# Moving weight sums, plane stores and a Silu, and a last norm by columns, in a hybrid decoder layer

## The chip, the core and the metric

The kernel runs on one core of one Trainium2 chip. The metric is the device time of one execution in microseconds (us). Engines are named as in the profile: PE is TensorE's matmul and PEld its weight load, DVE is VectorE, ACT is ScalarE, POOL is GpSimd, SP is SyncE, which issues most DMAs. A small q behind a name (ACTq, SPq) is that engine's issuing of DMAs.

## The reference

One decoder layer over 1024 tokens with 1024 features, all in float32: a half-step SwiGLU (FFN1), a mixer of three gated branches, and a second half-step SwiGLU (FFN2), each between two RMS norms.

```python
def swiglu(u, w_in, w_out):
    gate, up = jnp.split(u @ w_in, 2, axis=-1)      # w_in 1024 x 5632
    return (jax.nn.silu(gate) * up) @ w_out         # w_out 2816 x 1024
...
h = x
f1 = swiglu(rms_norm(h, ffn1_pre_g), ffn1_w_in, ffn1_w_out)
h = h + 0.5 * rms_norm(f1, ffn1_post_g)
u = rms_norm(h, mix_pre_g)
p_rwkv, p_swa, q_mem, gate_logits = _split(u @ w_in, IN_SIZES)
y_a = rwkv7_mix(p_rwkv, ...)                  # recurrence over tokens, 8 heads of 64
y_b = sliding_window_gqa_sinks(...)           # window of 128, 8 query and 2 key heads
y_c = memory_cross_attention(...)             # 256 memory tokens, 4 heads of 128
g_a, g_b, g_c = _split(sigmoid(gate_logits + gate_b), (D, D, D))
merged = g_a * (y_a @ w_branch[0]) + g_b * (y_b @ w_branch[1]) + g_c * (y_c @ w_branch[2])
h = h + rms_norm(merged @ w_out, mix_post_g)
f2 = swiglu(rms_norm(h, ffn2_pre_g), ffn2_w_in, ffn2_w_out)
h = h + 0.5 * rms_norm(f2, ffn2_post_g)
```

## The kernel before

Activations lie with features on the 128 partitions and tokens along the free dimension, in two halves of 512 tokens. Every product is made of three matmuls (`mm3`, L330 to L332): each factor is split into a high part (`w_hi`, a cast on ACT, L264) and a low part (`w_lo`, a subtraction on DVE, L266), and high x high, high x low and low x high are added in PSUM. Weights come as 128x512 tiles `w_raw` of 256 KB, loaded on SP in the order in which they are used (`raw`, L255); five such tiles exist, and eight operands (pairs of `w_hi` and `w_lo`) are made ahead (`prefetch`).

Both feed-forward products use a Strassen-like scheme with seven products of half-size blocks instead of eight. For the first product (`ffn_in`) the factors of the activations are sums of quarters (`factors_*`), and the sums of the input weights are made on DVE in place (`operands`, L285 to L291). Each of the 22 pairs j, a strip of the gate and one of the up half, takes seven block products, b11, b21, t2, t1, t3, b22 and t4 in the code. For the first 9 pairs of FFN1 and the first 13 of FFN2 (`FIRST`) the first two of the seven, which need only half of the tokens, are made early (`ffn_in_gate`) while the rest of the norm is still being made; their results `m1` and `g` go to DRAM (`first_d`) and are loaded again in the pair itself (L599, L600). These are called ahead pairs (`ahead`): they have five products left, 60 matmuls, where a later pair has 84. In a pair, `u1` and `m5` (L608) read PSUM on DVE in an ahead pair and on ACT in a later one; `up` (L621) reads it on DVE; then come the Silu of the second half `g1` (L625), for an ahead pair also the Silu of the reloaded `g0` (L629), and the products with `up` and `m1`. TensorE cannot add the next product to a bank before `u1`, `m5` or `up` has read it.

For the second product (`ffn_outs`) the seven forms of the hidden activations are made from every two pairs (`out_forms`, L567 to L570) and go to DRAM (`form_d`). Its weights need sums of blocks as well. There are 11 sets (`KP`), each of four DVE instructions on four 256 KB tiles `ws` (L555 to L558); a set is loaded on SP from the output weights (L553) and stored to `sum_d` (L560), from where `ffn_outs` later loads it like other weights. One set is made in every even pair.

In the RWKV stage (`rwkv_prep`) DVE and ACT prepare six planes for each of four head pairs while TensorE projects; `raw` copies (L825) on ACT bring a projection from PSUM. Four PSUM banks hold two projections, so TensorE starts the next but one only when the copy of the older one has been made. The planes and `bonus` go to DRAM from ACT's queue (L978, L979), as 64-element pieces.

Attention runs block by block (`attention`); in between, a generator (`filling`) supplies projections of the gates and the first two branches, so that TensorE has matmuls while ACT and DVE do the softmax. Within the tile framework a scheduler orders the instructions of each engine; `high_priority`, `issue_after` and `keep_in_program_order` bind it.

The end of the kernel is the last norm of FFN2 on the last 256 tokens (`post_norm`, `inverse_root`): squares are summed on ACT and DVE, the mean over features is made by two matmuls with a 1/D matrix on 256 columns, ACT and DVE form the inverse root on 128x256 elements, and eight feature tiles are scaled (L752), added to the residual (L755, three of them on POOL) and stored.

Of the kernel before, what the change touches and what calls it, by code (L numbers as in the profile page):

```python
# [17 lines left out]
P = 128  # L18
# [189 lines left out]
class Builder:  # L208
# [41 lines left out]
    def raw(self, ahead):  # L250

        used = self.raw_pos - len(self.raw_ready)
        while self.raw_pos < min(used + 1 + ahead, len(self.raws)):
            t = self.wpool.tile([P, KH, P], F32, tag="w_raw", name="w_raw", bufs=RAWS)
            self.send(t, self.raws[self.raw_pos])  # L255
            self.raw_ready.append(t)
            self.raw_pos += 1
        return self.raw_ready.pop(0)
# [99 lines left out]
    def rstd(self, sqs, width, pool, n, between):  # L358
        nc = self.nc
        V = nc.vector  # L360
        keep = self.tc.keep_in_program_order
        nb = n // P
        ps = self.psum("ps_ms")
        for j in range(nb):
            for i, sq in enumerate(sqs):
                keep(nc.tensor.matmul(ps[:, j : j + 1], sq[:, j * P : (j + 1) * P], self.ones, start=i == 0, stop=i == len(sqs) - 1))
        m, y, hm, q = (pool.tile([P, 4], F32, tag="rs" + t, name="rs" + t, bufs=2)[:, :nb] for t in "myhq")
        with self.tc.high_priority(offset=self.lead):
            V.tensor_scalar(m, ps[:, :nb], 1.0 / width, EPS, ALU.mult, ALU.add)
            V.tensor_scalar(y.bitcast(I32), m.bitcast(I32), 1, None, ALU.logical_shift_right)  # L370
            V.tensor_scalar(y.bitcast(I32), y.bitcast(I32), -1, 0x5F3759DF, ALU.mult, ALU.add)
            V.tensor_scalar(hm, m, -0.5, None, ALU.mult)
            for _ in range(3):
                V.tensor_tensor(q, y, y, ALU.mult)
                V.tensor_tensor(q, q, hm, ALU.mult)
                V.scalar_tensor_tensor(y, q, 1.5, y, ALU.add, ALU.mult)
        between()
        out = self.psum("ps_rs")
        with self.tc.high_priority(offset=self.lead):
            for j in range(nb):  # L380
                keep(nc.tensor.matmul(out[:, j * P : (j + 1) * P], y[:, j : j + 1].broadcast_to([P, P]), self.ident, start=True, stop=True))
        return out, y

# [140 lines left out]
    def ffn_in(self, f, x, form_d, first_d, parts, norm):  # L524

        nc, V = self.nc, self.nc.vector
        with self.tc.tile_pool(reuse_waits="tile", name="ffn_in", bufs=2) as pool:
# [11 lines left out]
            stored = None  # L539
# [7 lines left out]
    def out_sums(self, f, q, pool, loads_behind, sums_behind):  # L547

        nc, V = self.nc, self.nc.vector
        a11, a12, a21, a22 = a = [pool.tile([P, KH, P], F32, tag="ws", name="ws", bufs=4) for _ in range(4)]  # L550
        with self.tc.issue_after(loads_behind.ins):
            for n, t in enumerate(a):
                nc.sync.dma_start(t, self.io[f + "_out"][n, q])  # L553
        with self.tc.issue_after(sums_behind.ins):
# [4 lines left out]
        for n, t in zip(SUMS, (a22, a11, a21, a12)):  # L559
            nc.sync.dma_start(self.sum_d[f][SUMS.index(n), q], t)  # L560

    def out_forms(self, i, first, second, pool, form_d):
# [8 lines left out]
        for n, t in (("b11", b11), ("b21", b21), ("t2", t2), ("t3", t3), ("t4", t4), ("t1", b12), ("b22", b22)):  # L571
            stored = nc.sync.dma_start(form_d[B_FORM[n], i], t)
        return stored
# [16 lines left out]
    def ffn_in_pair(self, f, j, pool, first_d):  # L590
# [4 lines left out]
        if ahead:  # L595
# [3 lines left out]
            self.reload = nc.sync.dma_start(m1, first_d[j, 0])  # L599
# [25 lines left out]
        nc.scalar.activation(g1, g1, ACT.Silu)  # L625
        V.tensor_tensor(g1, g1, up, ALU.mult)
        self.product(px, self.take(name, j), fs["t4"], last=True)
        if ahead:
            nc.scalar.activation(g0, g0, ACT.Silu)  # L629
# [111 lines left out]
    def post_norm(self, acc, part, gcol, xr, pool, save=None):  # L741
# [5 lines left out]
        end = save is self.io["out"]  # L747
        with self.tc.high_priority(offset=self.urgent if end else 0):
            sq = self.sum_squares(xs[KH:] + xs[:KH] if h else xs, pool)
        rs = self.inverse_root(sq, pool, self.between if end else None)  # L750
        for k in range(KD):
            nc.vector.scalar_tensor_tensor(xs[k], xs[k], gcol(k), rs, ALU.mult, ALU.mult)  # L752

            e = nc.gpsimd if end and cols.stop == T and k in (0, 2, 4) else nc.vector
# [109 lines left out]
    def rwkv_prep(self, u, pool, pk_d, ab_d, bonus_d, att_d):  # L864
# [47 lines left out]
        for p in range(NPAIR):  # L912
# [61 lines left out]
            def bonus(p=p, parts=m_parts, m=m, planes=(*bk, at, r, v)):  # L974
                for h, cols, ps in self.head_sums(*parts):
                    V.tensor_tensor(ch(m[:, cols]), ch(ps), planes[4][:, h * 8 : (h + 1) * 8, :], ALU.mult)
                for i, x in enumerate(planes):
                    nc.scalar.dma_start(pk_d[:, :, p, i * C : (i + 1) * C].rearrange("c p t -> p c t"), x)  # L978
                nc.scalar.dma_start(bonus_d[p], m)  # L979
# [198 lines left out]
    def filling(self, u, pool, gate_d, y_d):  # L1178

        for g in range(GATES_EARLY, 22):  # L1180
            ps = {h: self.psum("pgate") for h in (0, 1)}
            yield from self.project_steps(self.strip("win", 24 + g), u, ps)
            self.gate_out(g, ps, pool, gate_d)

# [10 lines left out]
        for g, p in zip(gs, ps):  # L1195
            self.gate_out(g, p, pool, gate_d)
        self.mg = self.u_by_half(F32)
# [188 lines left out]
    def branch(self, i, y, pool, gate_d, mg, halves=(0, 1), between=None):  # L1386

        for q in range(4):
            w = self.strip("wb", 4 * i + q)
            parts = [(h,) for h in halves] if q == 0 or q == 3 and between else [halves]  # L1390
            for n, part in enumerate(parts):
# [3 lines left out]
                yield from self.branch_strip(i, q, w, y, pool, gate_d, mg, part)  # L1395
        return out if between else None
# [31 lines left out]
    def mixer(self, u, cp, close_raws, att_d, gate_d, km_d, vm_d):  # L1428
# [11 lines left out]
        with tc.tile_pool(reuse_waits="tile", name="gates", bufs=2) as gp:  # L1440
# [15 lines left out]
            with tc.tile_pool(reuse_waits="tile", name="att", bufs=1) as ap, tc.tile_pool(name="attw", bufs=2) as pool:  # L1456
# [36 lines left out]
                def turn_values():  # L1493
# [7 lines left out]
                    self.yin = opened.enter_context(tc.tile_pool(reuse_waits="tile", name="yin", bufs=4))  # L1501

# [4 lines left out]
                for _ in self.fills:  # L1507
                    pass
                opened.close()
# [40 lines left out]
    def build(self):  # L1550
        nc, tc, io = self.nc, self.tc, self.io
        with contextlib.ExitStack() as outer, tc.tile_pool(reuse_waits="tile", name="consts", bufs=1) as cp, \
# [4 lines left out]
            self.log_table = False  # L1557
# [10 lines left out]
            self.eps = cp.tile([P, 64], F32, name="eps")[:, :1]  # L1568
            nc.vector.memset(self.eps, EPS * D / P)
            self.ident = cp.tile([P, P], F32, name="ident")  # L1570
# [127 lines left out]
```

## Time and profile before

| what | value |
|---|---|
| median of 3 runs | 2316.37 us (2315.68 to 2319.36) |
| the profiled execution | 2317.92 us, span 2316.2 us |
| mean granted clock of TensorE | 0.994 |
| instructions | 33482 |
| DMA | 417.68 MB, mean 180 GB/s |

FFN1's gates and ahead pairs lie between about 40 and 232 us, its later pairs up to about 470, the RWKV stage between about 760 and 930, attention with the fills between about 1200 and 1510, FFN2's gates and ahead pairs between about 1640 and 1914, and the last norm in the final 15 us.

In the lines of the profile, a group shows the line, engine, operation and tiles (out<-in), the count, the busy time and the mean length of one in ns, and the idle time before it with what ended it. A row of a timeline begins with the start and the length in us, and ends with the idle time before it in brackets. Consecutive instructions of one engine overlap at their ends, so the distance between two starts is less than the length of one.

### The profile page before, as it was taken

To read this page: it belongs to the slowest core of one execution; us is meant where nothing else is said; L and a number is where in the kernel's file an instruction comes from. 1 tells how busy PE (TensorE), PEld (TensorE's weight loads), DVE (VectorE), ACT (ScalarE), POOL (GpSimd) and SP (SyncE) were. 2 spreads that over 40 slices of the span, in tenths; PEclk is the share of its full clock that TensorE was granted. 3 is DMA by queue.
4 is the path that set the end of the run, shared out by engine and by line. 5 is a ranking of instruction groups with operands and counts; after the bars stand their busy time and mean duration, and the time that the engine had idled before them with its cause. 6 is when DMAs were issued, how large, how long until landed. Compare 5 with 4: busy or idle time off the path is not lost. (4 is left out here: it accounts for less than half of the span.)

```text
span 2316.2 us, 33482 instructions
## 1 busy us (share of the span) xinstructions
PE 2263.1 (98%) x11914; PEld 1848.4 (80%) x11914; DVE 1657.5 (72%) x2683; ACT 995.3 (43%) x1844; POOL 94.5 (4%) x134
## 2 busy tenths in 40 slices
PE   8999999999999999999999999999999999999997
PEld 6778888888888777888878887778878778888887
DVE  6988666665688776895645466575999886666576
ACT  5523333454555553223444454335653223345452
POOL 0000000000000000001300000240000000000000
PEclk9999999999999999999999999999999999999998
DMA  7477545586654447325435434554557774558663
GB/s 281 164 258 246 178 151 167 172 294 200 191 164 156 108 119 185 120 100 178 148 128 175 133 97 162 178 186 162 179 191 243 248 243 165 168 193 264 211 194 111
DMA packets 280777, 417.68 MB, mean 180 GB/s; under 512 B 82305, under 2 KB 104321, under 8 KB 280353
## 3 DMA queue, kind: packets, MB, share of 16 engines
q1 hardware_dynamic: 231552, 388.20, 50.9%
q10 hardware_dynamic: 49056, 27.34, 4.3%
q8 instruction: 94, 1.54, 0.3%
q14 instruction: 75, 0.61, 0.1%
HBM read 284.89 MB, written 129.50 MB: 179 GB/s over the span
## 5 line engine op out<-in xcount | busy, mean ns | idle before, releaser
L264 ACT CAST w_hi<-w_raw 128x512 fp32r<-128x512 f32 x594 | 366.7, 619 | 718.8 <-PE px L331 140.4
L266 DVE TENSOR_TENSOR w_lo<-w_raw,w_hi 128x512 fp32r<-128x512 f32 x594 | 414.8, 700 | 214.2 <-ACT w_hi L264 190.4
L331 PE MATMUL po<-u,w_hi 128*128 128x512 f32 (+1 forms) x476 | 181.0, 380 | 0.0
L330 PE MATMUL po<-u,w_hi 128*128 128x512 f32 (+1 forms) x476 | 181.0, 380 | 0.0
L332 PE MATMUL po<-u,w_lo 128*128 128x512 f32 (+1 forms) x476 | 181.0, 380 | 0.0
L330 PE MATMUL pgate<-u,w_hi 128*128 128x512 f32 x384 | 155.5, 405 | 0.0
L332 PE MATMUL pgate<-u,w_lo 128*128 128x512 f32 x384 | 151.3, 394 | 0.0
L331 PE MATMUL pgate<-u,w_hi 128*128 128x512 f32 x384 | 149.8, 390 | 0.0
L330 PE MATMUL px<-f,w_hi 128*128 128x512 f32 x352 | 138.8, 394 | 8.1 <-DVE up L621 4.8
L330 PE MATMUL pz<-u,w_hi 128*128 128x512 f32 x352 | 138.2, 393 | 6.1 <-DVE m L608 5.2
L330 PE MATMUL px<-u,w_hi 128*128 128x512 f32 x352 | 137.2, 390 | 2.9 <-ACT w_hi L264 1.5
L331 PE MATMUL pz<-u,w_hi 128*128 128x512 f32 x352 | 137.9, 392 | 0.0
L332 PE MATMUL pz<-u,w_lo 128*128 128x512 f32 x352 | 137.9, 392 | 0.0
L331 PE MATMUL px<-f,w_hi 128*128 128x512 f32 x352 | 137.2, 390 | 0.0
L332 PE MATMUL px<-f,w_lo 128*128 128x512 f32 x352 | 137.1, 389 | 0.0
L332 PE MATMUL px<-u,w_lo 128*128 128x512 f32 x352 | 137.0, 389 | 0.0
L331 PE MATMUL px<-u,w_hi 128*128 128x512 f32 x352 | 137.0, 389 | 0.0
L413 DVE TENSOR_TENSOR u<-hid,u 128x512 fp32r<-128x512 f32 x114 | 78.4, 690 | 47.1 <-ACT u L412 46.1
L332 PEld LDWEIGHTS po<-u,w_lo 128*128 128x128 f32 x476 | 89.5, 188 | 17.1
L331 PEld LDWEIGHTS po<-u,w_hi 128*128 128x128 f32 x476 | 89.5, 188 | 17.0
L330 PEld LDWEIGHTS po<-u,w_hi 128*128 128x128 f32 x476 | 89.5, 188 | 16.9
L412 ACT CAST u<-hid 128x512 fp32r<-128x512 f32 x114 | 70.7, 620 | 65.3 <-DMA hid<-form_d 57.2
(358 smaller groups left out, 5139.3 us busy)
## 6 DMA issues: line engine op xcount, KB each, us to landing
w_raw<-in_ffn_in SPq DMA_DIRECT2D x220, 256.0 KB
hid<-form_d SPq DMA_DIRECT2D x154, 256.0 KB
w_raw<-in_win SPq DMA_DIRECT2D x112, 256.0 KB
ws<-in_ffn_out SPq DMA_DIRECT2D x88, 256.0 KB
form_d<-g SPq DMA_DIRECT2D x88, 256.0 KB
ffn_sum_d<-ws SPq DMA_DIRECT2D x88, 256.0 KB
w_raw<-ffn_sum_d SPq DMA_DIRECT2D x88, 256.0 KB
form_d<-h SPq DMA_DIRECT2D x66, 256.0 KB
```

Source lines behind the costliest of these rows:

```text
L264: self.nc.scalar.copy(hi, x)
L266: self.nc.vector.tensor_tensor(lo, x, hi.bitcast(F32), ALU.subtract)
L330: mm(out, wh, xh, start=first, stop=False, **kw)
L331: mm(out, wh, xl, start=False, stop=False, **kw)
L332: mm(out, wl, xh, start=False, stop=last, **kw)
L412: self.nc.scalar.copy(hi, x)
L413: self.nc.vector.tensor_tensor(lo, x, hi.bitcast(F32), ALU.subtract)
```

## The change

It has five parts. FFN1's sets of weight sums are made in pairs 9 to 19, one per pair, and no longer in every even pair from the first on. FFN2's sets are made during attention and the branches: `sums_beside` is a generator with a pool of seven tiles, of which one step (`unit`) is taken behind each gate and each quarter of a branch from then on. A step makes the sums of the set loaded before and loads the next. In both, the loads are bound behind the weight load issued last (`self.loaded`). The Silu of the reloaded gate is issued behind the Silu of the pair's second half. The RWKV planes and the bonus are stored from SP's queue. The last norm sums squares over features by matmuls with a column of ones, which leave two columns of 128 tokens, forms the root on 128x2 elements, and spreads it by matmuls with the identity (`last_root`); the last tile's square is kept apart from the others' sum, and four of the eight additions are on POOL.

```diff
-            for i in range(KP):
-                *first, made = self.ffn_in_pair(f, 2 * i, pool, first_d)
-                self.out_sums(f, i, pool, stored or self.reload, made)
-                *second, _ = self.ffn_in_pair(f, 2 * i + 1, pool, first_d)
-                stored = self.out_forms(i, first, second, pool, form_d)
+            pairs = []
+            for j in range(KF):
+                *pair, made = self.ffn_in_pair(f, j, pool, first_d)
+                pairs.append(pair)
+                if f == "ffn1" and FIRST[f] <= j < FIRST[f] + KP:
+                    self.sums_made(f, j - FIRST[f], self.sums_loads(f, j - FIRST[f], pool, 4), made)
+                if j % 2:
+                    self.out_forms(j // 2, *pairs[-2:], pool, form_d)
+    def sums_loads(self, f, q, pool, bufs):
+        a = [pool.tile([P, KH, P], F32, tag="ws", name="ws", bufs=bufs) for _ in range(4)]
+        with self.tc.issue_after(self.loaded.ins):
+            for n, t in enumerate(a):
+                self.nc.sync.dma_start(t, self.io[f + "_out"][n, q])
+        return a
+    def sums_beside(self, pool):
+        for q in range(KP):
+            a = self.sums_loads("ffn2", q, pool, 7)
+            yield
+            self.sums_made("ffn2", q, a)
+    def unit(self):
+        if self.units:
+            next(self.units, None)
...
-        nc.scalar.activation(g1, g1, ACT.Silu)
+        silu = nc.scalar.activation(g1, g1, ACT.Silu)
...
-            nc.scalar.activation(g0, g0, ACT.Silu)
+            with self.tc.issue_after(silu.ins):
+                nc.scalar.activation(g0, g0, ACT.Silu)
...
-                    nc.scalar.dma_start(pk_d[:, :, p, i * C : (i + 1) * C].rearrange("c p t -> p c t"), x)
-                nc.scalar.dma_start(bonus_d[p], m)
+                    nc.sync.dma_start(pk_d[:, :, p, i * C : (i + 1) * C].rearrange("c p t -> p c t"), x)
+                nc.sync.dma_start(bonus_d[p], m)
...
+    def last_root(self, sqs, pool):
...
+        for j in range(nb):
+            for i, sq in enumerate(sqs):
+                keep(nc.tensor.matmul(m[:, j : j + 1], sq[:, j * P : (j + 1) * P], self.ones, start=i == 0, stop=i == len(sqs) - 1))
+        with self.tc.high_priority(offset=self.lead):
+            keep(S.activation(y, m, ACT.Ln, scale=1.0 / D, bias=self.eps_mean))
+            keep(S.activation(y, y, ACT.Exp, scale=-0.5))
+            V.tensor_scalar(h, m, -0.5 / D, -0.5 * EPS, ALU.mult, ALU.add)
+            V.tensor_tensor(q, y, y, ALU.mult)
+            V.tensor_tensor(q, q, h, ALU.mult)
+            V.scalar_tensor_tensor(y, q, 1.5, y, ALU.add, ALU.mult)
+            for j in range(nb):
+                keep(nc.tensor.matmul(out[:, j * P : (j + 1) * P], y[:, j : j + 1].broadcast_to([P, P]), self.ident, start=True, stop=True))
+        return out[:, : nb * P]
...
-            e = nc.gpsimd if end and cols.stop == T and k in (0, 2, 4) else nc.vector
+            e = nc.gpsimd if last and k in (0, 2, 4, 6) else nc.vector
...
             self.gate_out(g, ps, pool, gate_d)
+            self.unit()
...
+                    self.units = self.sums_beside(opened.enter_context(tc.tile_pool(reuse_waits="tile", name="osum", bufs=7)))
```

More of the change, by code (lines that the diff above doesn't have):

```diff
@@ L598, in ffn_in_pair @@
             g0 = pool.tile([P, TH], F32, tag="gate", name="g", bufs=6)
-            self.reload = nc.sync.dma_start(m1, first_d[j, 0])
+            nc.sync.dma_start(m1, first_d[j, 0])
             nc.sync.dma_start(g0, first_d[j, 1])
@@ L1196, in filling @@
             self.gate_out(g, p, pool, gate_d)
+            self.unit()
         self.mg = self.u_by_half(F32)
@@ L1508, in mixer @@
                     pass
+                assert next(self.units, None) is None
                 opened.close()
```

37 lines of the change are left out of this document (23 added, 14 removed).

## The prediction

> **What bounds the kernel now.** I read the page's busy times first, then the waits of TensorE (PE), then the table of stretches around each wait.
>
> ```profile
> PE 2263.1 (98%) x11914; PEld 1848.4 (80%) x11914; DVE 1657.5 (72%) x2683; ACT 995.3 (43%) x1844; POOL 94.5 (4%) x134
> ```
>
> TensorE is busy almost throughout, so only time in which it waits, or runs at a lower clock, can be won. Its waits are few (engine, line waited for, releaser: us in total, times, longest):
>
> ```profile
> PE pr L330 <- ACT raw L825: 6.0, 2, 3.8
> PE pz L330 <- DVE m L608: 5.2, 1, 5.2
> PE px L330 <- DVE up L621: 4.8, 8, 1.3
> PE px L330 <- DVE u L608: 3.1, 2, 2.8
> ```
>
> Small waits hide in the busy share, so I count matmuls by stretch (stretch, length, then PE, PEld, DVE, ACT, POOL busy with counts, granted clock, DMA share, GB/s):
>
> ```profile
> 58.00:116.00 58.00, 56.87 (x247) 46.06 (x248) 55.04 (x91) 29.64 (x52) 0.00 (x0) 1.00 0.50 164
> 116.00:174.00 58.00, 53.99 (x234) 43.29 (x233) 51.14 (x84) 17.11 (x29) 0.00 (x0) 1.00 0.79 259
> 174.00:232.00 58.00, 56.77 (x250) 47.03 (x251) 51.85 (x84) 17.57 (x29) 0.00 (x0) 1.00 0.73 245
> 290.00:348.00 58.00, 58.00 (x257) 48.04 (x256) 37.43 (x60) 21.24 (x36) 0.00 (x0) 1.00 0.43 148
> 1740.00:1798.00 58.00, 57.86 (x248) 47.39 (x246) 52.97 (x86) 17.31 (x30) 0.00 (x0) 0.97 0.77 257
> 1798.00:1856.00 58.00, 55.13 (x239) 44.39 (x240) 49.31 (x79) 16.34 (x28) 0.00 (x0) 1.00 0.73 249
> 1856.00:1914.00 58.00, 56.77 (x246) 45.58 (x245) 51.54 (x83) 17.66 (x30) 0.00 (x0) 1.00 0.72 245
> ```
>
> An undisturbed stretch of a feed-forward stage (290 to 348) does 257 matmuls in 58 us, 0.226 us each. The first, second and third rows, FFN1's "ahead" pairs, lack 10, 23 and 7: 40 x 0.226 = 9.0 us. The last three, FFN2's, lack 9, 18 and 11: 8.6 us. In both stages VectorE (DVE) is busy for 85 to 95% of the time and DMA moves 245 GB/s or more; in the undisturbed one DVE has 65% and DMA 148 GB/s. An ahead pair issues 60 matmuls (13.5 us), a later pair 84 (19 us), while DVE has nearly the same to do. So the ahead pairs are where DVE is too much.
>
> **FFN1's and FFN2's sums.** One set of weight sums is four DVE instructions:
>
> ```profile
> 1740.51 1.89 DVE L266 TENSOR_TENSOR w_lo<-w_raw,w_hi 128x512 fp32r<-128x512 f32 x3
> L555 DVE TENSOR_TENSOR ws<-ws x22: 682/685/693, 122.1 to 2069.8; 128x512 f32<-128x512 f32 x22
> L285 DVE TENSOR_TENSOR w_sum<-w_raw 128x512 f32<-128x512 f32 x9 | 6.2, 688 | 6.6 <-DMA w_raw<-in_ffn_in 6.6
> L285 DVE TENSOR_TENSOR w_sum<-w_raw 128x512 f32<-128x512 f32 x12 | 8.3, 692 | 11.8 <-DMA w_raw<-in_ffn_in 11.7
> ```
>
> Three back-to-back instructions of this shape take 1.89 us: starts are 0.60 apart (the 685 ns overlap). An ahead pair has five lo parts, four sums of its own weights, seven steps on results and two of the four form steps: 18 x 0.60 = 10.8 us. With a set of weight sums it is 22 x 0.60 = 13.2 of 13.5 us, and the waits for weight loads (6.6 us over nine pairs of FFN1, 11.7 over twelve of FFN2) come on top. That is why TensorE falls behind in every second pair. The change takes five of FFN1's 11 sets and seven of FFN2's out of the ahead pairs, with eight 256 KB transfers each, so both the DVE work and the DMA load that delays w_raw shrink. The reloaded gate's Silu, put behind the other Silu of the pair, removes ScalarE's (ACT) waits for the reload:
>
> ```profile
> ACT g L629 <- DMA g<-first_d: 10.9, 7, 2.3
> ```
>
> These are off TensorE's path mostly (w_hi is made eight operands ahead), so I give that edit nothing of its own. FFN1: of 9.0 us I take 6.5 as recovered (the rest is start-up before the first set of sums). FFN2: of 8.6 us about 1.5 is the halved clock after the wait at 1732 (below), leaving 7.1, of which I take 5. What is late next there is TensorE's own rate. Bounds: nothing, if the w_raw loads set the pace, and 16.1 together.
>
> VectorE in FFN1's ninth ahead pair, before (ws the weight sums, u, m, up what TensorE's next products wait for):
>
> ```order
> L608 TENSOR_TENSOR u_1863<-px,m_1842 128x512
> L266 TENSOR_TENSOR w_lo<-w_raw,w_hi 128x512
> L555 TENSOR_TENSOR ws<-ws 128x512
> L556 TENSOR_TENSOR ws<-ws 128x512
> L608 TENSOR_TENSOR m_1882<-pz,m_1842 128x512
> L266 TENSOR_TENSOR w_lo<-w_raw,w_hi 128x512
> L557 TENSOR_TENSOR ws<-ws 128x512
> L285 TENSOR_TENSOR w_sum<-w_raw 128x512
> L558 TENSOR_TENSOR ws<-ws 128x512
> L621 TENSOR_TENSOR up<-px,m_1882 128x512
> ```
>
> The same pair in the changed kernel (g and h are steps of the forms for the second product, w_sum the sums of FFN1's input weights):
>
> ```order
> L649 TENSOR_TENSOR u_1926<-px,m_1901 128x512
> L266 TENSOR_TENSOR w_lo<-w_sum,w_hi 128x512
> L611 TENSOR_TENSOR g<-g 128x512
> L612 TENSOR_TENSOR h_1888<-g,h_1886 128x512
> L649 TENSOR_TENSOR m_1944<-pz,m_1901 128x512
> L266 TENSOR_TENSOR w_lo<-w_raw,w_hi 128x512
> L662 TENSOR_TENSOR up<-px,m_1944 128x512
> ```
>
> Between u and up stand five instructions and no longer eight, so up can come 1.8 us sooner.
>
> Where FFN1's sums go, pairs of 19 us, DVE has 37.43 of 58 us to do; every pair instead of every second one adds 1.2 us per pair, which fits. The ws loads now wait for the store of their buffer, with w_raw loads behind them on SyncE; prefetched operands cover that. I count 0; if the cover fails, 1.3 us (the longest wait for up above) in a few pairs.
>
> The wait at 1732 to 1738, between FFN2's gates and its first ahead pair, has no sums ahead of it:
>
> ```profile
> 1732.00:1738.00 6.00, 0.80 (x4) 0.41 (x3) 6.00 (x11) 2.49 (x5) 0.00 (x0) 0.89 0.26 87
> 1738.00:1743.00 5.00, 5.00 (x13) 3.89 (x13) 4.40 (x8) 2.70 (x5) 0.00 (x0) 0.50 0.27 92
> ```
>
> VectorE is busy for all 6 us: it works off the factor splits. The change keeps their order but puts u behind them, just ahead of m. I count 0, between 1 lost and 5 won.
>
> **RWKV plane stores.** Before, ACT issues 24 stores between its copies (third column: us):
>
> ```profile
> 796.91 0.34 ACTq L979 DMA_DIRECT2D bonus_d<-m  x1
> 831.54 2.83 ACTq L979 DMA_DIRECT2D bonus_d<-m  x1
> 834.41 1.07 ACT L825 COPY raw<-pr 128x512 f32<-128x512 f32 x2 [1.66 <-issue]
> 876.89 1.20 ACTq L979 DMA_DIRECT2D bonus_d<-m  x1
> 878.14 1.07 ACT L825 COPY raw<-pr 128x512 f32<-128x512 f32 x2 [0.97 <-issue]
> 835.00:840.00 5.00, 4.95 (x15) 3.91 (x16) 3.78 (x3) 1.85 (x3) 0.00 (x0) 0.66 0.49 177
> 880.00:885.00 5.00, 5.00 (x16) 3.94 (x16) 3.09 (x3) 1.36 (x2) 0.00 (x0) 0.67 0.58 183
> ```
>
> An issue that took 0.34 us at 796 took 2.83 and 1.20 at 831 and 876, right ahead of the two raw copies for which TensorE waited 6.0 us in total. After each wait the clock stood at 0.66 and 0.67 for 5 us: 1.7 + 1.65 = 3.35 us more, 9.35 in all. On SyncE these stores delay w_raw loads, which have 24 matmuls (5.4 us) per operand and up to 13 operands in hand. ScalarE ahead of the second copy, before (pk_d and bonus_d the stores, raw the copy):
>
> ```order
> L904 ACT_TABLE_LOAD
> L978 DMA pk_d<-bk 128x16x64
> L264 CAST w_hi<-w_raw 128x512
> L906 ACTIVATE ep<-sz 128x1024
> L978 DMA pk_d<-r 128x16x64
> L907 ACTIVATE sz<-sz 128x1024
> L264 CAST w_hi<-w_raw 128x512
> L908 COPY wc<-ep 128x16
> L978 DMA pk_d<-v 128x16x64
> L979 DMA bonus_d<-m 128x1024
> L825 COPY raw<-pr 128x512 x2
> ```
>
> The same place in the changed kernel:
>
> ```order
> L950 ACT_TABLE_LOAD
> L871 COPY raw<-pr 128x512 x2
> L952 ACTIVATE ep<-sz 128x1024
> L953 ACTIVATE sz<-sz 128x1024
> L954 COPY wc<-ep 128x16
> L264 CAST w_hi<-w_raw 128x512
> L871 COPY raw<-pr 128x512
> L264 CAST w_hi<-w_raw 128x512
> L871 COPY raw<-pr 128x512
> ```
>
> The stores are gone, but a w_hi cast, which waits for TensorE, still stands ahead of each of the two raw copies at the end. So I take 5 of 9.35, between 3 lost (TensorE's small products now stand earlier and can wait for ACT) and 9.35 won. The Trainium skill (DMA: Bandwidth & Descriptors, Issuing engines are not separate DMA queues) speaks against more: all queues share 16 DMA engines, and another issuer saves only issuing time. By that rule the gain would be 2.83 + 1.20 - 2 x 0.34 = 3.35 us and the sum 1.65 smaller; the trace agrees so far that the excess is issue time. On the clock, the wait before 880 was about 2.2 us of the 6.0 and lowered it. The Trainium skill (TensorE: Matmul & The Clock Gate, The HAM clock gate) gives an idle window of about 3.4 us for that; by it the wait at 876 would have cost no clock and the two waits would be worth 1.65 less, but the row shows that it did.
>
> **Last norm by columns.** Before (start, us):
>
> ```profile
> 2301.84 0.42 ACT L422 ACTIVATE sq<-acc 128x256 f32<-128x256 f32 x1 [3.10 <-DVE acc L707]
> 2306.74 1.75 DVE L752 SCALAR_TENSOR_TENSOR acc<-acc,post,rs 128x256 f32<-128x256 f32 x3
> L366 PE MATMUL ps_ms<-ones,mem_ss x8: 167/250/250, 20.4 to 21.1; 128*128 128x1 f32 x8
> L130 ACT ACTIVATE st<-st 128x8 f32<-128x8 f32 x8 | 1.6, 196 | 2.8 <-DVE st L129 2.8
> L374 DVE TENSOR_TENSOR rsq<-rsy 128x2 f32<-128x2 f32 x3 | 0.5, 154 | 0.0
> L381 PE MATMUL ps_rs<-ident,rsy x4: 272/275/275, 28.6 to 29.0; 128*128 128x128 f32 x4
> 2312.84 0.42 DVE L755 TENSOR_TENSOR acc<-acc,x_re 128x256 f32<-128x256 f32 x1
> ```
>
> From the last square's end (2302.26) to the first scaling (2306.74) are 4.5 us. The new chain: column matmuls 0.6, Ln and Exp 2 x 0.2, three small DVE steps 0.5, spreading matmuls 0.9, five changes of engine at about 0.1: 2.9. That wins 1.6, and the fourth addition on GpSimd takes 0.4 from DVE's last stretch: 2.0, between 1 and 2.8.
>
> **FFN2's sums in attention and branches.** 11 sets, 44 x 0.60 = 26 us of DVE, and 88 transfers:
>
> ```profile
> 1218.00:1276.00 58.00, 57.29 (x289) 48.49 (x288) 30.17 (x55) 25.81 (x60) 1.96 (x3) 1.00 0.56 176
> 1450.00:1508.00 58.00, 57.71 (x277) 46.40 (x276) 29.02 (x52) 17.33 (x40) 17.43 (x12) 1.00 0.56 187
> ```
>
> DVE has about half its time free and DMA 0.4 of its share there. It works in order, so a ws step whose load is late holds back scores and softmax steps for which TensorE waits. Nothing excludes a cost up to that of a set in the ahead pairs, 16.1/12 = 1.3 us, 15 in all; a gain is excluded, since nothing leaves the stage. I take 2, nearer to nothing, because of the free half.
>
> **Sum.** 6.5 + 5 + 0 + 5 + 2 - 2 = 16.5 us off the profiled execution's 2317.9 us (span 2316.2) is 2301.4; that execution was 1.5 above the median of 2316.4, so 2299.9 in the median's terms. Call it 2300. About 0.2%, 4.6 us, is what a measurement of this kernel can tell from no change.
>
> **Rivals.** First: the new order in the RWKV stage brings its waits back, and the term is 0: 2305. For it, the w_hi casts ahead of raw; against it, the 2.83 us issue is gone. Second: weight loads, not sums, set the ahead pairs' pace, and of 11.5 only 3 come: 2308.5. For it, the waits for w_raw; against it, eight transfers fewer per set. Third, slower: in attention each set is fully exposed on DVE, 4 x 0.60 = 2.4 us, 26.4 in all instead of 2: 2324. It decides from (16.5 + 2)/11 = 1.7 us a set on. For it, VectorE's strict order there with ws loads queued behind buffer waits on SyncE; against it, the free half. That the change does not do as it says is excluded by the orders above.
>
> **Chances.** Forecast 0.60 (its own range 2293 to 2307), first 0.15, second 0.13, third 0.12. Faster by over 0.2% (below 2311.8) is all of the first two and most of the second rival: 0.80; within 0.2%: 0.09, from the second rival's and the third's near ends; slower 0.11. The range reaches from 2291 (12 us of the ahead pairs' 16.1, 8 of the RWKV waits, 2.8 of the norm, attention at 0: 23 less, and 2 for the 1732 wait) to 2313, the second rival with attention at three times its price (2312.5).
>
> **What would show it.** Right: near 257 matmuls in each 58 us of the ahead pairs; no wait for raw of 3.8 us; first scaling some 3 us behind the last square; no new PE wait between 1200 and 1510. Wrong: ws steps waiting for DMA in attention with TensorE behind, PE still waiting for up and m in the ahead pairs, or new waits for raw, ss or rk in the RWKV stage.

## The result and the profile after

| | median | lowest to highest | runs |
|---|---|---|---|
| before | 2316.37 us | 2310.64 to 2319.88 | 9 |
| after | 2310.04 us | 2306.17 to 2312.33 | 9 |

The ratio is 0.9977, with a 95% interval of 0.9967 to 0.9987: by it 5 us are won (the medians differ by 6.3), where 16.5 were forecast. The change makes the kernel faster, as forecast, but by about a third of what was forecast. The profiled execution took 2310.06 us, its span is 2308.4 us. Of all the executions behind the ratios in this document one, of the run with four sets below, took 3230 us at a mean granted clock of 0.654 and is left out of its ratio.

To see where the time went I take the start of each TensorE product in the trace after, subtract the start of the same product before, and follow this difference through the kernel. It changes only where a stage became longer or shorter. Worked out so, for this profile and for a second one of the same kernel that was taken with the experiments (us, minus is won):

| stage (us of the trace before) | forecast | after | second profile |
|---|---|---|---|
| start, to 58 | 0 | -2.1 | -0.5 |
| FFN1's ahead pairs, 58 to 290 | -6.5 | -5.8 | -4.8 |
| FFN1's later pairs and on, to 757 | 0 | +0.6 | +0.1 |
| RWKV stage, 757 to 920 | -5 | -8.8 | -8.7 |
| chain and first gates, to 1240 | 0 | -1.0 | -0.6 |
| gates and attention, 1240 to 1450 | +2 (with the next row) | +11.0 | +11.8 |
| last branches, 1450 to 1600 | | +5.1 | +3.7 |
| FFN2's first pairs, 1700 to 1920 | -5 | -3.4 | -2.5 |
| the rest of FFN2, to 2220 | 0 | +0.3 | +0.4 |
| end | -2 | -3.7 | -4.0 |
| span | -16.5 | -7.8 | -5.1 |

FFN1's ahead pairs come out near the forecast, FFN2's at half to two thirds of it. These are the stretches of the changed kernel (stretch, length, PE, PEld, DVE, ACT, POOL busy with counts, granted clock, DMA share, GB/s):

```profile
58.00:116.00 58.00, 58.00 (x256) 47.54 (x255) 56.83 (x94) 29.20 (x51) 0.00 (x0) 1.00 0.47 155
116.00:174.00 58.00, 56.66 (x249) 46.14 (x248) 50.75 (x82) 18.43 (x32) 0.00 (x0) 1.00 0.62 199
174.00:232.00 58.00, 57.95 (x257) 47.67 (x256) 42.31 (x68) 18.96 (x33) 0.00 (x0) 1.00 0.49 167
1740.00:1798.00 58.00, 56.71 (x250) 46.31 (x248) 46.48 (x75) 16.44 (x28) 0.00 (x0) 1.00 0.60 198
1798.00:1856.00 58.00, 57.04 (x251) 46.74 (x251) 48.13 (x77) 17.78 (x30) 0.00 (x0) 1.00 0.54 178
1856.00:1914.00 58.00, 57.56 (x255) 47.36 (x254) 47.12 (x76) 18.52 (x31) 0.00 (x0) 1.00 0.49 163
```

256, 249 and 257 matmuls stand where 247, 234 and 250 stood, and 250, 251 and 255 where there were 248, 239 and 246. From 116 us on, VectorE has less to do in every row (42.3 for 51.9 us in the third), and the DMA traffic has fallen from 245 GB/s and more to between 163 and 199.

The RWKV stage's waits for `raw` are gone altogether. TensorE's longest waits from 757 to 925 us in the changed kernel (waiting line, releaser: us, times, longest), and the stage's projections before and after (tile view; the last two times are the first and the last start):

```profile
PE ab L1014 <- ACT w_hi L264: 1.2, 1, 1.2
PE ss L901 <- DVE n_lo L437: 0.7, 1, 0.7
```

```profile
L330 PE MATMUL pr<-u,w_hi x224: 388/389/628, 682.9 to 891.7; 128*128 128x512 f32 x112
L330 PE MATMUL pr<-u,w_hi x224: 388/389/500, 675.6 to 875.3; 128*128 128x512 f32 x112
```

From 208.8 us they have come down to 199.7, and the longest matmul from 628 to 500 ns, since the clock no longer drops: its mean from 757 to 925 us was 0.98 before and is 1.00 now.

What was won there, and more, is given back among the branch products. Their first to last start, before and after:

```profile
L330 PE MATMUL pb<-u,w_hi x128: 387/389/504, 1409.4 to 1514.8; 128*128 128x512 f32 x128
L330 PE MATMUL pb<-u,w_hi x128: 387/389/504, 1395.0 to 1512.6; 128*128 128x512 f32 x128
```

105.4 us have become 117.6. TensorE's longest waits from 1190 to 1560 us after, and one of VectorE's in the same stretch:

```profile
PE ptr L96 <- DVE sc L136: 6.6, 4, 3.8
PE pb L330 <- DVE gin L1466: 2.6, 2, 1.6
PE ptr L96 <- ACT yo L1421: 1.9, 2, 1.4
```

```profile
DVE ws L586 <- DMA ws<-in_ffn_out: 20.9, 9, 3.9
```

None of the first three stood in the trace before at more than 0.3 us. VectorE stands still for 20.9 us in front of the first addition of a set (L586), for a load that has not landed: 8.8 us at five sets ahead of the branch products, 12.1 us at the last four, among them. Behind these four in VectorE's order stand the softmax steps. Ahead of TensorE's longest wait VectorE's timeline reads (start, length; in brackets the idle time before):

```profile
1394.15 1.89 DVE L123 SCALAR_TENSOR_TENSOR sc<-sc,wmask 128x512 f32<-128x512 f32 x3 [1.60 <-PE sc L93]
1399.38 0.69 DVE L586 TENSOR_TENSOR ws<-ws 128x512 f32<-128x512 f32 x1 [3.34 <-DMA ws<-in_ffn_out]
1399.99 0.69 DVE L123 SCALAR_TENSOR_TENSOR sc<-sc,wmask 128x512 f32<-128x512 f32 x1
...
1401.19 2.28 DVE L126 TENSOR_REDUCE st<-sc 128x8 f32<-128x2048 f32 x1
...
1407.75 0.69 DVE L586 TENSOR_TENSOR ws<-ws 128x512 f32<-128x512 f32 x1 [1.05 <-DMA ws<-in_ffn_out]
...
1412.81 2.19 DVE L136 TENSOR_SCALAR sc<-sc,st 128x256 f32<-128x256 f32 x8
```

For this wait the last of the masked scores (L123) and their maximum (L126) come 3.3 us later, and another 1.05 is lost before the scaling (L136). Eight additions of sums, of about 0.6 us each, stand in the same sequence. TensorE needs the scaled scores, waits 3.8 us, and then runs at a lower clock:

```profile
1413.31 3.10 PE L96 MATMUL ptr<-ident,sc 128*128 128x128 f32 x15 [3.82 <-DVE sc L136]
1413.00:1418.00 5.00, 4.70 (x26) 4.13 (x28) 2.60 (x9) 2.35 (x4) 0.00 (x0) 0.66 0.95 350
1437.00:1442.00 5.00, 5.00 (x34) 3.98 (x34) 1.22 (x5) 1.68 (x4) 0.00 (x0) 1.00 0.83 284
```

At 0.66 over 5 us that is 1.7 us more. After the second of these waits (1.7 us, ended at 1435.86) the clock stays at 1.00.

The end: last square, then the first scalings (ACT, DVE).

```profile
2296.89 0.42 ACT L446 ACTIVATE sq<-acc 128x256 f32<-128x256 f32 x1 [3.10 <-DVE acc L749]
2300.11 1.26 DVE L798 SCALAR_TENSOR_TENSOR acc<-acc,post,ps_rs 128x256 f32<-128x256 f32 x3 [0.81 <-PE ps_rs L405]
```

From the square's end (2297.31) to the first scaling are 2.8 us; the forecast said 2.9, before the change it was 4.5.

### The profile page after: what moved, and what is told of

Its sections match the earlier page's. It is cut to its first block, busy times and chain, and to the rows that moved or that the text cites. A ratio compares the mean times of both kernels' runs of the same rounds, so it can differ in the third digit from the quotient of the medians.

```text
span 2308.4 us, 33523 instructions
## 1 busy us (share of the span) xinstructions
PE 2257.9 (98%) x11924; PEld 1848.0 (80%) x11924; DVE 1658.6 (72%) x2683; ACT 993.1 (43%) x1842; POOL 94.7 (4%) x135
```

## The experiments

Each run was timed against the kernel before on its own chip, so the ratios compare best. The stage losses quoted are worked out as in the table above. The theory: the sums beside attention cost so much because additions in VectorE's strict order wait for loads that come late, and this happens in the four last sets, which stand among the branch products. Rivals: VectorE's added work costs it, or the 88 transfers do, or something else in the change.

**Seven sets beside attention, four in FFN2's later pairs.**

```diff
-        for q in range(KP):
+        for q in range(7):
             a = self.sums_loads("ffn2", q, pool, 7)
...
-                if f == "ffn1" and FIRST[f] <= j < FIRST[f] + KP:
-                    self.sums_made(f, j - FIRST[f], self.sums_loads(f, j - FIRST[f], pool, 4), made)
+                q = j - FIRST[f] + {"ffn1": 0, "ffn2": 7}[f]
+                if 0 <= q < KP and j >= FIRST[f]:
+                    self.sums_made(f, q, self.sums_loads(f, q, pool, 4), made)
```

> The changed kernel, but of FFN2's 11 sets of weight sums only the first seven are made beside attention; the last four, which stood in the branches, are made in FFN2's pairs 13 to 16, behind each pair. Theory (the loss of 16 us lies in the four sets that stand among the branch products, where a late load holds up softmax steps on VectorE): the 16 us between the gates and the last branches vanish, the later pairs take four sets at no cost, and the time is 2310 - 16 = 2294. Rival (all eleven sets cost alike, about 1.5 us each): seven sets still cost 10, and the time is 2304. Second rival (the time goes to whatever stage takes the sums): 2310.

2301.17 us, ratio 0.9936 (0.9923 to 0.9950). The branch products take 106.9 us again, and TensorE's waits for `sc` fall from 6.6 to 0.8:

```profile
L330 PE MATMUL pb<-u,w_hi x128: 389/389/504, 1396.4 to 1503.3; 128*128 128x512 f32 x128
PE ptr L96 <- DVE sc L136: 0.8, 2, 0.5
```

From 1240 to 1450 us 1.8 us are lost in place of 11.0. The time is 7 us above the theory's 2294, partly because 2.8 us still go between 1450 and 1600; by its stages the four last sets are the ones that cost. This is the softmax sequence of the same block as above, from the first masked scores to the first scaling, without a set in it:

```profile
1395.49 2.48 DVE L123 SCALAR_TENSOR_TENSOR sc<-sc,wmask 128x512 f32<-128x512 f32 x4 [1.61 <-PE sc L93]
...
1406.93 2.19 DVE L136 TENSOR_SCALAR sc<-sc,st 128x256 f32<-128x256 f32 x8
```

It takes 11.4 us; in the changed kernel it took 18.7 (1394.15 to 1412.81).

**Only these four beside attention, the first seven in FFN2's later pairs.**

```diff
+        for _ in range(7):
+            yield
+        for q in range(7, KP):
-        for q in range(KP):
             a = self.sums_loads("ffn2", q, pool, 7)
```

> The other half of the seven-set run: only the last four sets stand beside attention, among the branch products, at the same places as in the changed kernel; the first seven are made in FFN2's pairs 13 to 19. If these four sets carry the loss: 9 to 11 us lost between 1240 and 1450 us and a time near 2309. If the loss needs all eleven (traffic or VectorE's backlog that builds up): 4 us or less lost there, and 2301.

2310.67 us, ratio 0.9975 (0.9963 to 0.9988): as slow as the changed kernel, with four sets instead of eleven. (The first addition of a set is on L587 in this run's numbering.)

```profile
L330 PE MATMUL pb<-u,w_hi x128: 387/389/504, 1393.5 to 1510.7; 128*128 128x512 f32 x128
PE ptr L96 <- DVE sc L136: 5.6, 2, 3.9
DVE ws L587 <- DMA ws<-in_ffn_out: 12.1, 4, 3.9
```

117.2 us for the branch products. 8.0 us are lost between 1240 and 1450, a little below the expected 9 to 11, and 2.7 more up to 1480: 2.7 us a set. The four sets wait 12.1 us for their loads, 3.0 each.

**The transfers without the additions.**

```diff
             yield
-            self.sums_made("ffn2", q, a)
+            for n, t in zip(SUMS, (a[3], a[0], a[2], a[1])):
+                self.nc.sync.dma_start(self.sum_d["ffn2"][SUMS.index(n), q], t)
```

> The changed kernel with the 88 transfers of FFN2's sums beside attention, but without the 44 additions: the four loaded blocks are stored as they came, so FFN2 runs on other weights. Theory (VectorE in order: additions that wait for their load, and the time that they take): without them no loss, 2294. Rival (the transfers delay the loads of gates and weights): the loss of 16 us stays, 2310. In between, the shift of the stage divides the 16 us.

2300.58 us, ratio 0.9935 (0.9922 to 0.9947): near the theory's end, though 6 us above its 2294. The branch products take 105.6 us and 2.3 us are lost between 1240 and 1450:

```profile
L330 PE MATMUL pb<-u,w_hi x128: 389/389/504, 1396.8 to 1502.4; 128*128 128x512 f32 x128
```

**The additions without the transfers.**

```diff
+        a = a11, a12, a21, a22 = self.sums_loads("ffn2", 0, pool, 7)
         for q in range(KP):
-            a = self.sums_loads("ffn2", q, pool, 7)
             yield
-            self.sums_made("ffn2", q, a)
+            V.tensor_tensor(a22, a21, a22, ALU.add)
...
```

> FFN2's sums back in the even ahead pairs as in the run above, and in attention the 44 additions alone, on four blocks that are loaded once, without the other 84 transfers; nothing uses their results. If the cost in attention is the waiting of additions for late loads (20.9 us of VectorE's waits), almost nothing is lost there: 2299, as the run without sums in attention. If it is the 26 us of VectorE's work at that place, whatever the loads do: 2299 + 16 = 2315.

2303.41 us, ratio 0.9949 (0.9937 to 0.9962); 0.4 us are lost between 1240 and 1450, with all 44 additions in this stretch. (L602 is the first addition of a set in this run's numbering.)

```profile
L330 PE MATMUL pb<-u,w_hi x128: 389/389/504, 1394.5 to 1500.0; 128*128 128x512 f32 x128
L602 DVE TENSOR_TENSOR ws<-ws 128x512 f32<-128x512 f32 x11 | 7.5, 681 | 0.9 <-DMA ws<-in_ffn_out 0.9
L602 DVE TENSOR_TENSOR ws<-ws x11: 656/684/693, 1265.4 to 1306.5; 128x512 f32<-128x512 f32 x11
```

The last row gives the first and the last start of these eleven: with no loads to wait for, the scheduler put all eleven sets between 1265 and 1309 us, among the gate products, and none among the branch products, where the loss was. So the run shows that the additions cost next to nothing there, and says nothing of their place among the softmax steps. Neither half costs more than 2.3 us; together they cost 11. The transfers alone are ruled out; whether it is the waiting for a load or the additions' place is left to the runs below. (The time is above 2299 since FFN2's first pairs took 2.7 us longer than before the change; the next run has that too.)

**FFN2's sums back in the even ahead pairs, the rest as changed.**

```diff
+                if f == "ffn2" and j % 2 == 0:
+                    self.loaded = stored or self.reload
+                    self.sums_made(f, j // 2, self.sums_loads(f, j // 2, pool, 4), made)
...
-                    self.units = self.sums_beside(...)
```

> The changed kernel, but FFN2's sums are back in the even ahead pairs, as before the change; all else of the change stays. Theory (the sums cost 16 us in attention and win 4.6 in the ahead pairs): 2310 - 16 + 4.6 = 2298 to 2299. Rival (the loss in attention comes from something else, such as the earlier arrival of the stage after the RWKV stage was shortened): the loss stays and the time is 2310 + 4.6 = 2315.

2305.21 us, ratio 0.9956 (0.9944 to 0.9969). Attention loses 0.2 us between 1240 and 1450, so the sums are the cause there; but 3.6 us are lost between 1450 and 1600 without any set beside attention. Divided at 1480, that stage holds two things. Up to 1480 the four profiles with the last four sets unheld among the branch products lose 2.3 to 2.8 us and every other profile 0.0, so this part belongs to the sums. Behind 1480 a loss comes and goes between kernels (-0.8 to 4.9; here 3.6) and was not pinned down. FFN2's first pairs are 3.8 us longer than before with the same sums (2.7 in the run above). Moving the sets is thus worth 2.7 + 3.4 to 3.8 + 3.4, or 6 to 7 us in FFN2, and something else in the change costs it about 3.

**Loads one set earlier, additions left to the scheduler.**

```diff
+        sets = [self.sums_loads("ffn2", 0, pool, 8)]
+        yield
         for q in range(KP):
-            a = self.sums_loads("ffn2", q, pool, 7)
+            if q + 1 < KP:
+                sets.append(self.sums_loads("ffn2", q + 1, pool, 8))
             yield
-            self.sums_made("ffn2", q, a)
+            self.sums_made("ffn2", q, sets.pop(0))
```

> The changed kernel with all eleven sets beside attention, at the same 44 places, but each set's loads issued one set earlier, before the additions of the set ahead of it (eight blocks for weights in place of seven, paid for with three in place of four for the branches' inputs). If the loss comes from additions that wait for a load which SyncE issued too late, the 11 us lost between the gates and 1450 us fall to 3 or less and the time is 2300 to 2302. If additions and transfers together cost it wherever the loads stand (more traffic, more work), 2310.

2313.89 us, ratio 0.9999 (0.9990 to 1.0008): worse than both forecasts. (The profiled execution took 2321.57 us, the longest of the twelve, so its stage losses may be high.) The edit did not do what it was meant to. The scheduler moved the additions forward too: beside attention they still lie 6 to 13 us behind the first load of their set (6 to 14 in the changed kernel), and the waits grew:

```profile
1422.15 1.19 SPq L578 DMA_DIRECT2D ws<-in_ffn_out  x2
...
1431.83 0.69 DVE L586 TENSOR_TENSOR ws<-ws 128x512 f32<-128x512 f32 x1 [6.73 <-DMA ws<-in_ffn_out]
...
DVE ws L586 <- DMA ws<-in_ffn_out: 26.0, 9, 6.7
```

It tells only that more waiting for loads (26.0 for 20.9 us) goes with more loss (14.3 for 11.0 us).

**Additions held behind the next strip's last step.**

```diff
-                yield from self.branch_strip(i, q, w, y, pool, gate_d, mg, part)
-            self.unit()
+                done = yield from self.branch_strip(i, q, w, y, pool, gate_d, mg, part)
+            self.unit(done)
...
-            self.sums_made("ffn2", q, a)
+            self.sums_made("ffn2", q, a, self.unit_behind)
```

> The changed kernel with all eleven sets beside attention, but from the branches on the four additions of a set are held behind VectorE's last step of the branch strip that follows their loads, so that the loads have a whole strip (some 11 to 22 us) in place of 5 to 7 us. If additions that wait for loads are the cost, VectorE's waits for these loads (20.9 us) fall by half or more and of the 11 us lost between 1240 and 1450 us less than 4 stay: 2301 to 2303. If the place of the additions among the softmax steps costs it without any wait: 2310.

2300.74 us, ratio 0.9936 (0.9918 to 0.9955), as the theory said. All eleven sets are made beside attention, 44 additions and 88 transfers, and the branch products take 104.8 us:

```profile
L330 PE MATMUL pb<-u,w_hi x128: 389/389/504, 1396.7 to 1501.5; 128*128 128x512 f32 x128
DVE ws L586 <- DMA ws<-in_ffn_out: 6.2, 5, 2.0
1392.00:1450.00 58.00, 57.50 (x324) 45.90 (x325) 45.55 (x95) 26.37 (x79) 0.00 (x0) 1.00 0.72 236
```

and here is a set between the same softmax steps (L133, L134, L136) as at 1410 us of the changed kernel, with no wait ahead of it; it is the only one of this run's last five that stands inside a softmax sequence:

```profile
1443.11 0.68 DVE L586 TENSOR_TENSOR ws<-ws 128x512 f32<-128x512 f32 x1
1443.83 0.69 DVE L587 TENSOR_TENSOR ws<-ws 128x512 f32<-128x512 f32 x1
1444.44 0.16 DVE L133 TENSOR_TENSOR st<-st 128x8 f32<-128x8 f32 x1
1444.55 0.69 DVE L588 TENSOR_TENSOR ws<-ws 128x512 f32<-128x512 f32 x1
```

In this run 1.9 us are lost between 1240 and 1450, with a DMA share of 0.72. So neither the work nor the traffic makes the loss by itself; it comes when the additions stand among the softmax steps before their loads have landed. How much of it is the waiting and how much the place is not fully separated, since the edit moved most sets out of the softmax sequences as well. What the traces show of the place: a sequence took 13.4 us with four additions in it and no wait (in this run, from 1432.50), 12.5 with three (in the changed kernel, from 1441.94, with a wait just ahead of it), and 12.7 with none (in the seven-set run, the same block). The two sequences of the changed kernel that hold a wait took 18.7 and 17.3 us where the seven-set run's took 11.4 and 10.4: some 14 us more, 8.3 of them waits for loads, with twelve additions among the steps.

**No sums moved: RWKV stores, last norm and later Silu alone, in the kernel before.**

```diff
-                    nc.scalar.dma_start(pk_d[...], x)
-                nc.scalar.dma_start(bonus_d[p], m)
+                    nc.sync.dma_start(pk_d[...], x)
+                nc.sync.dma_start(bonus_d[p], m)
...
+            with self.tc.issue_after(silu.ins):
+                nc.scalar.activation(g0, g0, ACT.Silu)
...
+        rs = self.last_root(sqs, pool) if last else ...
```

> The kernel before with the RWKV stores on SyncE, the last norm by columns and the later Silu, and no sums moved. From the stage shifts so far: RWKV stage 8.5 to 8.9 won, tail 2.0 to 2.8 won, so 2316 - 11 = 2305 if the later Silu is worth nothing. In the run with FFN2's sums back in the even ahead pairs, FFN2's ahead pairs were 3.9 us longer than before with the same sums; if that is the later Silu's doing, they are 3.9 longer here too and the time is 2309; if it is not, these pairs take as long as before.

2305.02 us, ratio 0.9961 (0.9949 to 0.9973). The RWKV stage wins 8.3 us, and of the edits of this run only the stores lie in it; the end wins 3.9. FFN1's ahead pairs win 2.3 and FFN2's first pairs lose 2.7, both with the sums where they were. The time agrees with the first expectation only because these two cancel: by its stages the later Silu does not seem to be free, which the next run tests.

**The Silu back, on the seven-set version.**

```diff
-            with self.tc.issue_after(silu.ins):
-                nc.scalar.activation(g0, g0, ACT.Silu)
+            nc.scalar.activation(g0, g0, ACT.Silu)
```

> The run with seven sets beside attention and four in FFN2's later pairs (ratio 0.9936, 2301), with the reloaded gate's Silu where it was before the change. If the later Silu is worth nothing: the same, 2301. If it costs the 3.9 us that the even-pair run suggests: 2297. If it removes waits of ScalarE that reached TensorE: later, 2303 or more.

2298.21 us, ratio 0.9935 (0.9922 to 0.9948); against the seven-set run's 0.9936 the times do not tell them apart, but the traces, one of each, do: FFN2's first pairs win 6.4 us in place of 4.0, FFN1's 5.3 in place of 5.2. The place is the start of FFN2's ahead pairs. TensorE's longest wait there, with the Silu back and then in the seven-set run with the later Silu:

```profile
PE pz L330 <- DVE m L650: 3.7, 1, 3.7
PE px L330 <- DVE u L650: 5.6, 1, 5.6
```

VectorE in the same two runs, the first two rows with the Silu back:

```profile
1716.74 0.70 DVE L650 TENSOR_TENSOR u<-px,m 128x512 f32<-128x512 f32 x1
...
1723.36 0.70 DVE L650 TENSOR_TENSOR m<-pz,m 128x512 f32<-128x512 f32 x1
...
1724.14 0.68 DVE L650 TENSOR_TENSOR u<-px,m 128x512 f32<-128x512 f32 x1
...
1725.34 0.68 DVE L650 TENSOR_TENSOR m<-pz,m 128x512 f32<-128x512 f32 x1
```

With the Silu back, u starts 6.6 us ahead of m, with factor splits between them, and TensorE can go on with the product that needs u alone; with the later Silu it stands behind the splits, 1.2 us ahead of m, and TensorE waits for it. An edit on ScalarE has moved an instruction on VectorE. In FFN1, where the run before won 2.3, this edit changed nothing (5.3 and 5.2).

**The changed kernel again.**

> The changed kernel itself once more, on the chip of the three runs above, as their base: ratio 0.9977, as before, with the stage shifts of its first profile: FFN1's ahead pairs -6 to -7, RWKV -9, attention and branches +16, FFN2's ahead pairs -3.5, tail -2.8. How far a second profile differs from the first shows how much of a stage's shift is the kernel's and how much the execution's.

2310.61 us, ratio 0.9982 (0.9974 to 0.9991). The second profile is in the first table: between two executions a stage's shift differs by up to 1.5 us.

**Five sets beside attention, six in FFN2's later pairs, Silu back.**

```diff
-        for q in range(KP):
+        for q in range(5):
...
+                q = j - FIRST[f] + {"ffn1": 0, "ffn2": 5}[f]
...
-            with self.tc.issue_after(silu.ins):
-                nc.scalar.activation(g0, g0, ACT.Silu)
+            nc.scalar.activation(g0, g0, ACT.Silu)
```

> A version meant to be faster: five sets beside attention (those among the gate products), six in FFN2's pairs 13 to 18, and the reloaded gate's Silu where it was before. Against the run with seven sets and that Silu (2298), the sixth and seventh set no longer stand where 2.9 us were lost between 1340 and 1450 us: 2295 to 2296. If the later pairs cannot take six sets: 2300.

2297.81 us, ratio 0.9912 (0.9896 to 0.9929): the fastest version run, though its interval still touches that of the run with seven sets and the Silu back. 0.2 us are lost between 1240 and 1450 and 8.5 won in FFN2's first pairs; its profile lost 3.8 between 290 and 757, 3.0 of it in one wait for a norm's square, which in this execution accounts for the missed 2295.

**No set beside attention, all in FFN2's later pairs.**

```diff
+                sets = [q] if f == "ffn1" else [2 * q, 2 * q + 1] if q < 2 else [q + 2]
+                for s in sets:
+                    if q >= 0 and s < KP:
+                        self.sums_made(f, s, self.sums_loads(f, s, pool, 4), made)
...
-                    self.units = self.sums_beside(...)
```

> No set beside attention; FFN2's pairs 13 to 21 make all eleven, the first two of them two sets each; the reloaded gate's Silu where it was before. If the later pairs have room for a set each (VectorE was busy for 37 of 58 us there): 2295 to 2297, with attention as before the change. If two sets in a pair are too much, or the last set comes too late for the products of the forms: 2300 or more.

2305.65 us, ratio 0.9952 (0.9937 to 0.9966): the second expectation. From 1240 to 1450 attention is as before the change, but 9.3 us are lost between 1920 and 2220, about half in the two pairs with two sets each, the rest where the second product begins:

```profile
2072.00:2130.00 58.00, 54.48 (x235) 43.20 (x234) 36.56 (x57) 29.15 (x51) 0.00 (x0) 1.00 0.84 280
```

## Why the prediction was wrong

- **FFN2's sums in attention: the failed step.** The prediction bounded this term by 0 and 15 us and took 2, "because of the free half" of VectorE. It came out at 13.6 and 14.6 us up to 1480 in two profiles, and at 16.1 and 15.5 with the loss behind that, which was not pinned down. The mechanism had been named, a ws step whose load is late in VectorE's strict order, and also the sign of it; the choice of the price was wrong. VectorE's free half does not bear on it: the additions cost 0.4 among the gate products, and 1.9 with all the transfers when most were held until their loads had landed. What counted is that a set's loads land after VectorE has come to its first addition, in nine of eleven sets and by up to 3.9 us, and how soon TensorE needs what stands behind it. Five sets waited 8.8 us ahead of the branch products, and 0.1 us was lost up to 1380; four waited 12.1 us among them, and the rest of the loss stands there.
- **The third rival** had that order at 2.4 us for each of eleven sets, from the additions' own time. The price was about 3 us, for four sets, and mostly for waiting. Its 2324 and the forecast's 2300 lie on either side of what happened.
- **That 2310 lies in the range, and next to the second rival's 2308.5, is luck.** The range's upper end was made of weight loads that set the ahead pairs' pace, and the ahead pairs won 9.2 and 7.3 us in the two profiles, not 3.
- **RWKV stores: mis-sized.** 5 was taken of 9.35; 8.3 to 8.9 came in every run. The fear that the w_hi casts ahead of `raw` would keep the waits was unfounded. The Trainium skill (DMA: Bandwidth & Descriptors, Issuing engines are not separate DMA queues) says that another issuer saves only issuing time, and the prediction's estimate by it was 3.35 us. The measurement is above that: an issue that stands ahead of a copy in ScalarE's order costs the copy's waiter (6.0 us) and the clock (0.66 and 0.67 over 5 us) as well.
- **FFN1's sums: right.** 4.6 to 5.8 for 6.5 in the runs that moved them. Without moving any, these pairs won 2.3 in one run; of its edits only the later Silu lies there, but with the sums moved that Silu made no difference in FFN1, so how much is the sums' own is not settled.
- **FFN2's ahead pairs and the wait at 1732.** The sums were worth 6 to 7 where 5 was taken, but the wait, whose change was put at 0, grew from 5.2 to 6.2 us, and the later Silu, given "nothing of its own", was what moved u behind the splits: 2.4 to 2.7 us lost. The prediction saw that u had moved and did not ask which edit moved it.
- **Last norm: right.** 1.7 lie between the square and the first scaling, 1.6 in the sum. From the last square's end to the kernel's end 13.9 us became 11.1: 2.8, the upper bound of the term. The 0.9 and 1.1 us that the end won ahead of that square were not traced.
- **The clock.** A wait of 3.8 us at 1413 was followed by 0.66 over 5 us, one of 1.7 at 1436 was not. The Trainium skill (TensorE: Matmul & The Clock Gate, The HAM clock gate) gives an idle window of about 3.4 us; these two waits agree with it. The 2.2 us wait of the RWKV stage before, which 0.67 followed, does not, and there the measurement decides.

With the measured terms the sum is -5.8 - 8.8 + 16.1 - 3.4 - 3.7 and -2.2 for the start and the small stages: -7.8 us, the difference of the spans.

## What to carry to other kernels

Idle time of an engine says that more work fits, not that work which waits for a transfer fits: in a strict order an addition can cost the lateness of its load. So ask first when the load lands in that very stretch, and bind the consumer behind something that is later than that. Holding the additions behind a later step took the cost from 11 us to 1.9 with the same work and the same traffic, where issuing the loads earlier alone won nothing, since the scheduler moved the additions along. An experiment that takes the waits away can be moved by the scheduler too: before reading it, see where the instructions stand in its trace. Price every reordering edit by the instructions that it moves on other engines too: a Silu on ScalarE moved a PSUM read on VectorE and cost about 2.5 us.

## What the runs showed of the hardware

The loads of a set take longer than their issue tells. SyncE's issues of one set in the changed kernel, and its first addition on VectorE:

```profile
1413.70 2.64 SPq L578 DMA_DIRECT2D ws<-in_ffn_out  x2
1417.02 1.12 SPq L578 DMA_DIRECT2D ws<-in_ffn_out  x2
1423.85 0.69 DVE L586 TENSOR_TENSOR ws<-ws 128x512 f32<-128x512 f32 x1 [3.92 <-DMA ws<-in_ffn_out]
```

The last load was issued by 1418.14 and the addition could start 5.7 us later, while DMA moved 350 GB/s at a share of 0.95 (1413 to 1418) and 303 at 0.88 (1418 to 1423). At the nine additions that waited, this distance was 3.1 to 5.7 us; for the eleven sets of FFN1 in the same trace it is 7.9 to 19.9 us, and none of their additions waits. The same traffic is nearly harmless where nothing in a strict order waits for it: with the additions held, attention ran at a share of 0.72 with 1.9 us lost.

Issuing the 24 stores of the RWKV stage from ScalarE cost 8 to 9 us of a stage of 163, while from SyncE they cost nothing that the traces show. Only the 20 stores of planes are in 64-element pieces. The four of `bonus`, whose rows in `bonus_d` are 1024 elements long, are not, though the two issues of 2.83 and 1.20 us are theirs, each right behind the issue of a plane; why these two took so long is not shown.
